# The seven-product scheme moved from the down to the up projection of a convolutional feed-forward block

## The chip, the cores and the metric

The kernel runs on one core of a Trainium2 chip. A core has a matrix engine (TensorE, PE in the rows, with its weight loads as PEld), a vector engine (VectorE, DVE), a scalar engine (ScalarE, ACT), a general engine (GpSimd, POOL) and a queue engine (SyncE, SP) that issues the loads. The metric is the device time of one execution in microseconds.

## The reference, cut to what matters

Two layers, 512 tokens on a grid of 8 rows and 64 columns, width 1024. Each layer adds three branches to x: a mixer with two kinds of attention, cross attention over a memory, and the block that the change touches:

```
def conv_ffn(h, w_up, conv_w, conv_b, w_down):       # h (512, 1024), w_up (1024, 2*2816), w_down (2816, 1024)
    u = h @ w_up
    up = pad(u, one token on either side)
    u = up[:-2] * conv_w[0] + up[1:-1] * conv_w[1] + up[2:] * conv_w[2] + conv_b
    gate, val = split(u, 2)
    return (silu(gate) * val) @ w_down

x = x + conv_ffn(rms_norm(x, norm_ffn[l]), ...)      # last step of each of the two layers
```

Everything is float32.

## The kernel before, in words

**Layout.** All activations lie transposed: channels on the 128 partitions, the 512 tokens along a row. The 1024 channels of x are eight tiles `xT[0..7]`. Tokens are in grid order: the eight rows of a grid column lie together (token = column * 8 + row), so the neighbour in the text is 8 places further, except at a column's wrap-around.

**Products.** A float32 operand is split in two parts of a reduced format: `hi` is the rounded value (a cast, always on ACT), `lo` what is left of it (a subtraction, on DVE or POOL). A product is three matmuls, `hi*hi + hi*lo + lo*hi` (`mm3`, `gemm_T`). A weight block arrives as `raw` (three buffers, 512 KB each) by a DMA on SP's queue and is split by `emit_split`; a letter in `weights()` says which engine makes the low part ("P" POOL, "D" DVE, "S" goes to `combined`). `get_w` hands out the blocks in one fixed order and keeps two split ahead.

**The feed-forward block of a layer.** 22 channel blocks j of 128 gate and 128 value channels. For each, `up_project` makes two products over the eight k tiles (2 x 8 x 3 = 48 matmuls of 512 columns) in PSUM banks tagged `sc` and `tr` (two of each), and `up_finish` multiplies both by the norm's row factor `ffn.rep`, adds the convolution (ACT for the middle tap, four DVE steps for the neighbours, two of 504 columns and two of 7), takes SiLU and multiplies gate by value. `up_first` handles the first two blocks, while the statistics of the norm (`stat`, `spread`) are still under way.

The down projection goes in two parts. The channel blocks 0 to 15 go in four groups of four. For each group g and each of four output pairs (m, m+4), `down_halved` multiplies a 2 x 2 block matrix of weights by a 2 x 2 block matrix of activations (two halves of the four blocks by two halves of 256 tokens) with seven products in place of eight: 7 x 2 x 3 = 42 matmuls of 256 columns instead of 24 of 512. For that, `combined` forms four sums of weight quarters on POOL, and splits three quarters (low parts on `LO_A`, DVE) and four sums (low parts on `LO_S`, POOL); `halved` forms four sums of activation halves on DVE. The results are added to `xT` by seven DVE steps. The down products of a group follow five channel blocks behind (`BEHIND`). The blocks 16 to 21 are multiplied plainly at the end by `down` (layer 0, with the next norm's operands made on the way by `close`) and `down_last` (layer 1, with the final norm and the output).

**What sets the order.** Nothing is issued as it is written. `Tape` records each step with its engine, what it reads and writes, and an estimate of its time (`Step.times`). `Tape.plan` runs a list scheduler over the record: PE takes the earliest step of the program that can start, within a reach of 300 steps; the other engines take the step that is due first. The best of some rounds under disturbed times is played, and each engine then runs its list in order. All steps are issued in `play`, so that the profile gives line 395 for nearly all of them: rows are told apart by their tiles. `mm`, `sc` and `tr` are PSUM tags (four, two and two banks), `t` is a pool of 14 temporary rows, `r` one of 23 operand tiles, `raw`, `hi` and `lo` are weight tiles, `xg` the two big tiles of a norm's split operand.

The functions that the change touches:

Of the kernel before, what the change touches and what calls it, by code (L numbers as in the profile page):

```python
# [19 lines left out]
P = 128  # L20
# [12 lines left out]
N_HALVED = [16, 16]  # L33
UPS = [j + (0, 1, -1, 0)[j % 4] if j < max(N_HALVED) else j for j in range(NF)]
# [24 lines left out]
N_RAW, N_W, AHEAD, AHEAD_HELD, N_WARM, N_LATE, N_FIRST = 3, 4, 2, 5, 7, 4, (12, 22)  # L59

# [429 lines left out]
def encoder_kernel(ctx: ExitStack, tc: tile.TileContext, t: dict, out: list):  # L490
# [5 lines left out]
    LO_A, SUMS, LO_S = DVE, POOL, POOL  # L496
# [60 lines left out]
    def combined(raw):  # L557


        hi, lo = [wpool.tile([P, 6, P], F32R, tag=tag, name=nm(tag)) for tag in ("hi", "lo")]  # L560
        shi, slo = rtile((8, P)), rtile((8, P))
        quarter = raw.rearrange("p (n k) c -> p n k c", k=2)
        first, second = tmp((2, 2, P)), tmp((2, 2, P))
        ACT.copy(hi, raw[:, 0:6])
        LO_A.tensor_sub(lo, raw[:, 0:6], f(hi))
        SUMS.tensor_add(first, quarter[:, 0:2], quarter[:, 3:4].to_broadcast([P, 2, 2, P]))
        SUMS.tensor_add(second[:, 0], first[:, 0], quarter[:, 1])
        SUMS.tensor_add(second[:, 1], second[:, 0], quarter[:, 2])
        for v, c in ((first, slice(0, 4)), (second, slice(4, 8))):
            v = v.rearrange("p n k c -> p (n k) c")  # L570
            ACT.copy(shi[:, c], v)
            LO_S.tensor_sub(slo[:, c], v, f(shi[:, c]))
        parts = {}
        for i, n in enumerate(("11", "22", "12")):
            parts[n] = [(hi[:, 2 * i + k], lo[:, 2 * i + k]) for k in range(2)]
        for i, n in enumerate(("s3", "s1", "s2", "s4")):
            parts[n] = [(shi[:, 2 * i + k], slo[:, 2 * i + k]) for k in range(2)]
        return parts

    def emit_split(act=ACT, cuts=2):  # L580
        n = len(ready)
        key, src, nk, ncol, eng = plan[n]
        raw = raws[n]
        raws[n] = None
        if eng == "S":
            ready.append(combined(raw))
            return
# [84 lines left out]

    def load_parameters():
        SP.dma_start(par, t["par"])
        SP.dma_start(qkg, t["qkg"])
        SP.dma_start(gcol, t["gcol"])
# [55 lines left out]
    class Norm:  # L732
# [51 lines left out]
        def spread(self):  # L784
            self.rep = tpool.tile([P, self.n], F32, tag="rep", name=nm("rep"), bufs=1)
            if self.last is None:
# [105 lines left out]
    for l in range(DEPTH):  # L892
# [602 lines left out]
        def up_project(j, side):  # L1495
            pm = ps_t() if side else ps_s()
            gemm_T(pm, get_w(("up", j, side)), ffn.ops, range(KC), 0, KC - 1)
            return pm

        def up_first():  # L1500


            ws, us = [], []
            for side in range(2):
                ws.append(get_w(("up", 0, side)))
                us.append(ps_mm())
                gemm_T(us[side], ws[side], ffn.ops, range(KC - 1), 0, KC - 1)
            for side in range(2):
                gemm_T(us[side], ws[side], ffn.ops, [KC - 1], 0, KC - 1)
                if side == 0:  # L1510
                    ffn.stat()
            us1 = [up_project(UPS[1], 0)]
            ffn.spread()
            up_finish(0, us)
            us1.append(up_project(UPS[1], 1))
            up_finish(UPS[1], us1)

        def up(j):
            up_finish(j, [up_project(j, side) for side in range(2)])

        def up_finish(j, us):
            for side in range(2):
                DVE.tensor_mul(us[side], us[side], ffn.rep)
            cs = []
            for side in range(2):
                ch = side * NF + j
                u = us[side]
                w = [par[:, l, CW + i * 2 * NF + ch : CW + i * 2 * NF + ch + 1] for i in range(3)]
                cc = tmp()
# [11 lines left out]
            if j < N_HALVED[l]:  # L1541
                halved(j, cs[0])
                return
            acts[j] = rpair()
            ACT.copy(acts[j][0], cs[0])
            DVE.tensor_sub(acts[j][1], cs[0], f(acts[j][0]))

        H = S // 2
        quads, shared, waiting = {}, [], {}

        def halved(j, u):


            n = UPS.index(j)
            if n % 4 == 0:
                shared[:] = [rtile((2, 2, H))]
            if n % 2 == 0:
                waiting[n + 1] = u
                hl = shared[0][:, n // 2 % 2]
# [335 lines left out]
```

## Time and profile before

| | |
|---|---|
| median of three runs | 1309.4 us (1309.1 to 1310.06) |
| the profiled execution, span from first to last instruction | 1308.6 us, 0.8 us under the median |
| PE busy | 1300.8 us, 99%, 6981 matmuls |
| PEld busy | 1120.7 us, 86% |
| DVE busy | 1054.7 us, 81%, 2011 instructions |
| POOL busy | 807.4 us, 62%, 607 instructions |
| ACT busy | 740.1 us, 57%, 1396 instructions |
| DMA | 137.42 MB, 105 GB/s on the mean |

How to read it: rows of groups give engine, operation, `output<-inputs`, shapes and count, then the busy time in us and the mean of one in ns, then the idle time of that engine just before them and what ended it. Matmul records overlap, as matmuls are pipelined: what one costs in a stream is read from the distance between starts, or from a piece of the chain with its count, and not from the mean of its records. A row of the chain of waits gives start, length and count of a piece. The granted clock of TensorE is full (1.00) throughout.

### The profile page before, as it was taken

The numbers are of one execution on the slowest core, as the hardware profiler recorded it, in microseconds if no ns is written. First come the engines' busy times: TensorE is split into PE (matmuls) and PEld (weight loads), VectorE is DVE, ScalarE is ACT, GpSimd is POOL, SyncE is SP. The second block draws the span as 40 slices with busy tenths as digits, with TensorE's granted clock in tenths as the row PEclk, the third lists the DMA queues.
The fourth block names the chain that finished last, engine by engine and source line by source line (L and its number), as shares of the span: only waits on it lengthen the run. The fifth ranks groups of instructions, "written<-read, shape, count | busy, mean of one in ns | idle before, by whom it ended". The sixth has DMA issues, their size and how long they took to land.

```text
span 1308.6 us, 19680 instructions
## 1 busy us (share of the span) xinstructions
PE 1300.8 (99%) x6981; PEld 1120.7 (86%) x6981; DVE 1054.7 (81%) x2011; ACT 740.1 (57%) x1396; POOL 807.4 (62%) x607
## 2 busy tenths in 40 slices
PE   9999999999999999999999999999999999999998
PEld 7898888888888888888888988888888888888897
DVE  8679996766999998987545898966769999989864
ACT  7777686555545444444537767865645445444442
POOL 4465867627666677773736657774466667777650
PEclk9999999999999999999999999999999999999999
DMA  8752313314323333332355422232133233333321
GB/s 284 217 146 51 111 49 97 97 37 115 94 78 115 111 97 97 101 115 91 105 161 178 127 67 82 65 113 82 49 113 99 96 97 102 108 97 98 102 92 65
DMA packets 42898, 137.42 MB, mean 105 GB/s; under 512 B 5040, under 2 KB 8496, under 8 KB 42800
## 3 DMA queue, kind: packets, MB, share of 16 engines
q1 hardware_dynamic: 42224, 135.51, 34.5%
q8 instruction: 55, 0.90, 0.3%
q10 hardware_dynamic: 576, 0.66, 0.1%
q14 instruction: 43, 0.35, 0.1%
HBM read 126.18 MB, written 2.10 MB: 98 GB/s over the span
## 4 chain that ended last, share of the span: by engine, by line
PE 96%; DMA 1%; POOL 1%; DVE 0%; issue 0%; SPq 0%; ACT 0%; POOLq 0%; DVEq 0%
PE mm L395 50%; PE sc L395 25%; PE tr L395 21%; POOL lo L395 1%; DMA t<-in_rope 1%; DMA r<-r 0%; DMA xT<-in_w 0%; POOL t L395 0%; SPq L395 0%; DVE t L395 0%; DVE s L395 0%; POOL r L395 0%; ACT hi L395 0%; DVE r L395 0%; ACT xg L395 0%
## 5 line engine op out<-in xcount | busy, mean ns | idle before, releaser
L395 POOL TENSOR_TENSOR lo<-raw,hi 128x512 fp32r<-128x512 f32 (+2 forms) x236 | 438.3, 1871 | 303.9 <-ACT hi L395 303.2
L395 ACT CAST hi<-raw 128x512 fp32r<-128x512 f32 (+2 forms) x276 | 219.9, 817 | 185.6 <-PE sc L395 70.0
L395 PE MATMUL mm<-r,hi 128*128 128x512 f32 (+1 forms) x928 | 244.8, 344 | 0.0
L395 PE MATMUL sc<-xg,hi 128*128 128x512 f32 (+1 forms) x740 | 228.8, 390 | 0.5 <-ACT xg L395 0.4
L395 PE MATMUL tr<-xg,hi 128*128 128x512 f32 x672 | 207.1, 389 | 0.0
L395 PEld LDWEIGHTS mm<-r,hi 128*128 128x128 f32 x928 | 162.5, 189 | 21.6
L395 PE MATMUL mm<-r,lo 128*128 128x256 f32 (+1 forms) x496 | 164.7, 332 | 0.0
L395 PEld LDWEIGHTS sc<-xg,hi 128*128 128x128 f32 x740 | 136.6, 188 | 28.2 <-ACT xg L395 0.8
L395 PE MATMUL mm<-r,r 128*128 128x256 f32 (+1 forms) x1064 | 159.2, 291 | 0.0
L395 PEld LDWEIGHTS tr<-xg,hi 128*128 128x128 f32 x672 | 126.0, 188 | 26.1
L395 PEld LDWEIGHTS mm<-r,r 128*128 128x128 f32 x1064 | 142.0, 192 | 3.7
L395 POOL TENSOR_TENSOR r<-t,r 128x512 fp32r<-128x512 f32 x80 | 118.1, 1480 | 42.6 <-ACT r L395 42.2
L395 PE MATMUL sc<-xg,lo 128*128 128x512 f32 (+1 forms) x370 | 143.3, 388 | 0.0
L395 ACT CAST r<-t 128x512 fp32r<-128x512 f32 (+1 forms) x164 | 94.4, 588 | 85.0 <-DVE t L395 68.6
L395 PE MATMUL tr<-xg,lo 128*128 128x512 f32 x336 | 130.7, 389 | 0.0
L395 DVE TENSOR_TENSOR xT<-xT,mm 128x256 f32<-128x256 f32 (+1 forms) x216 | 115.5, 554 | 11.5 <-PE mm L395 5.3
L395 PE MATMUL mm<-xg,hi 128*128 128x512 f32 (+1 forms) x386 | 121.5, 393 | 0.0
L395 DVE TENSOR_TENSOR t<-t,t 128x512 f32<-128x512 f32 (+1 forms) x110 | 114.8, 1063 | 4.9 <-ACT t L395 2.2
L395 PE MATMUL mm<-hi,xg 128*128 128x512 f32 (+1 forms) x384 | 108.4, 358 | 0.0
L395 POOL TENSOR_SCALAR t<-t,s 128x512 f32<-128x512 f32 (+1 forms) x112 | 67.5, 619 | 64.7 <-DVE s L395 59.0
L395 PEld LDWEIGHTS mm<-r,lo 128*128 128x128 f32 x496 | 93.9, 189 | 9.5
L395 DVE TENSOR_TENSOR r<-t,r 128x512 fp32r<-128x512 f32 (+1 forms) x84 | 80.0, 972 | 8.3 <-ACT r L395 8.0
(140 smaller groups left out, 2431.6 us busy)
## 6 DMA issues: line engine op xcount, KB each, us to landing
raw<-in_w SPq DMA_DIRECT2D x207, 512.0 KB, 3.6
r<-r SPq DMA_DIRECT2D x30, 256.0 KB, 3.6
r<-in_bias SPq DMA_DIRECT2D x16, 384.0 KB, 4.9
raw<-in_w SPq DMA_DIRECT2D x8, 384.0 KB, 3.0
r<-in_memT SPq DMA_DIRECT2D x4, 512.0 KB, 7.5
xT<-in_w SPq DMA_DIRECT2D x7, 256.5 KB, 4.7
r<-in_w SPq DMA_DIRECT2D x9, 128.0 KB, 4.2
t<-in_memT SPq DMA_DIRECT2D x4, 256.0 KB, 6.4
```

Of the source, the lines that this page charges most:

```text
L395: call(*args, **kwargs)
```

## The change

- The seven-product scheme leaves the down projection. `down_grouped` multiplies the same groups plainly: for each output pair two banks of 12 matmuls of 512 columns (24), and two additions to `xT`.
- It comes to the up projection of the channel blocks 6 to 21. Block matrix on the left: the weights of gate and value (one dimension) by the lower and upper four k tiles (the other). On the right: the two k halves by the two halves of 256 tokens. Seven products of 4 k tiles x 3 matmuls of 256 columns, 84 in place of 48 of 512. The products accumulate in turns in two banks (`val` and `gate`); between them ACT copies partial results out and DVE adds them. The last product and the finish of a block are put off into the next block (`finish_up`). The value half comes out negated, which the taps in `minus` take back.
- The right-hand operands are built once per layer by `operands`, from x, the gain and the norm's factor (so that no multiplication by `rep` follows in these blocks). Until they are there, the channel blocks 0 to 5 (`N_PLAIN`) go the plain way, with the multiplication.
- A weight block of gate and one of value are loaded as two mixed halves ("A", "B") and become three quarters and four sums of 512 columns in `combined`; all seven low parts are on DVE (`LO_S` goes from POOL to DVE), the four sums on POOL. The down weights now go the plain way, low part on POOL. The plain up weights of the blocks 1 and 2 go to DVE.
- Within the block the tokens are in natural order (line by line), so that a neighbour is one place further and the convolution needs two DVE steps instead of four. The norm's operand is written with a stride, and so are the activations for the down projection, which go back to grid order.
- The activations of the blocks 0 to 15 (but 2 and 3) are kept in the two `xg` tiles, which hold the norm's operand until the plain pairs are done.

The diff, cut to its core:

```diff
-N_HALVED = [16, 16]
-UPS = [j + (0, 1, -1, 0)[j % 4] if j < max(N_HALVED) else j for j in range(NF)]
+N_GROUPED = 16
+N_PLAIN = 6
+def behind(n):
+    return [] if n < N_PLAIN else range(0 if n == N_PLAIN else n - BEHIND, min(n - BEHIND + 1, N_GROUPED))
...
-    LO_A, SUMS, LO_S = DVE, POOL, POOL
+    LO_A, SUMS, LO_S = DVE, POOL, DVE
...
+    def combined(first, second, early):
+        parts = {}
+        for n, v in (("11", first[:, 0:4]), ("12", second[:, 4:8]), ("22", first[:, 4:8])):
+            parts[n] = operand_of(v, rtile((8, P)), LO_A)
+        sums = {n: tmp((4, P)) for n in ("s3", "s1", "s2", "s4")}
+        SUMS.tensor_add(sums["s1"], first[:, 4:8], second[:, 0:4])
+        SUMS.tensor_add(sums["s3"], first[:, 0:4], second[:, 0:4])
+        SUMS.tensor_add(sums["s2"], sums["s3"], first[:, 4:8])
+        SUMS.tensor_add(sums["s4"], sums["s2"], second[:, 4:8])
+        for n, tag in (("s1", "hi"), ("s2", "lo"), ("s4", "hi"), ("s3", "lo")):
+            parts[n] = operand_of(sums[n], rtile((8, P)) if early else wtile(tag), LO_S)
         return parts
...
             hi, lo = self.ops[c]
+            if self.gcol == G_FFN:
+                hi, lo = (v.rearrange("p (r c) -> p c r", r=ROWS) for v in (hi, lo))
+                src = src.rearrange("p (c r) -> p c r", r=ROWS)
...
+        def operands():
+            for c in range(4):
+                xs = []
+                for k in (c, c + 4):
+                    v = tmp()
+                    DVE.scalar_tensor_tensor(lines(v), rows(xT[k]), par[:, l, G_FFN + k : G_FFN + k + 1], rows(ffn.psum),
+                                             op0=ALU.mult, op1=ALU.mult)
+                    xs.append(v)
...
+                ACT.copy(pair(base[0]), b)
+                POOL.tensor_sub(pair(base[1]), b, f(pair(base[0])))
+                ACT.copy(base[2][:, i], a[:, :H])
+                DVE.tensor_sub(base[2][:, 2 + i], a[:, :H], f(base[2][:, i]))
...
+                POOL.tensor_sub(one[:, 0], a[:, :H], a[:, H:])
+                DVE.scalar_tensor_tensor(one[:, 1], one[:, 0], -1.0, b[:, H:], op0=ALU.mult, op1=ALU.subtract)
+                POOL.tensor_sub(two[:, 0], b[:, H:], a[:, H:])
+                DVE.scalar_tensor_tensor(two[:, 1], one[:, 1], -1.0, b[:, :H], op0=ALU.mult, op1=ALU.subtract)
+                hi, lo = rtile((4, H)), rtile((4, H))
+                for n, v in ((0, one), (2, two)):
+                    ACT.copy(hi[:, n : n + 2], v)
+                    DVE.tensor_sub(lo[:, n : n + 2], v, f(hi[:, n : n + 2]))
...
         def up(j):
-            up_finish(j, [up_project(j, side) for side in range(2)])
+            gate, val = ps_s(), ps_t()
+            x, y, v = val[:, :H], gate[:, :H], gate[:, H:]
+            sums, p5 = tmp((2, H)), tmp((H,))
+            product(x, w["11"], "11", True)
+            ACT.copy(sums[:, 0], x)
+            product(y, w["12"], "21", True)
+            finish_up()
+            product(v, w["s1"], "t1", True)
+            ACT.copy(p5, v)
+            product(x, w["s2"], "t2", False)
+            ACT.copy(sums[:, 1], x)
+            product(v, w["s4"], "22", False)
+            DVE.tensor_add(gate, gate, sums.rearrange("p n q -> p (n q)"))
+            product(x, w["s3"], "t3", False)
+            DVE.tensor_add(val[:, H:], x, p5)
+            def last():
+                product(x, w["22"], "t4", False)
+                up_finish(j, [gate, val], True)
+            left.append(last)
...
-                for wi, dst, src in (
-                    (w[0], slice(8, S), slice(0, S - 8)),
-                    (w[0], slice(1, 8), slice(S - 8, S - 1)),
-                    (w[2], slice(0, S - 8), slice(8, S)),
-                    (w[2], slice(S - 8, S - 1), slice(1, 8)),
-                ):
-                    DVE.scalar_tensor_tensor(cc[:, dst], u[:, src], wi, cc[:, dst], op0=ALU.mult, op1=ALU.add)
+                DVE.scalar_tensor_tensor(cc[:, 1:], u[:, : S - 1], w[0], cc[:, 1:], op0=ALU.mult, op1=ALU.add)
+                DVE.scalar_tensor_tensor(cc[:, : S - 1], u[:, 1:], w[2], cc[:, : S - 1], op0=ALU.mult, op1=ALU.add)
...
+            hi, lo = (rows(v) for v in acts[j])
+            ACT.copy(hi, lines(cs[0]))
+            DVE.tensor_sub(lo, lines(cs[0]), f(hi))
...
+        def down_grouped(g, m):
+            wh, wl = get_w(("down", g, m))
+            for i in range(2):
+                pm = ps_mm()
+                for k in range(4):
+                    mm3(pm, wh[:, 4 * i + k], wl[:, 4 * i + k], *acts[4 * g + k], k == 0, k == 3)
+                at = xT[m + 4 * i]
+                DVE.tensor_add(at, at, pm)
...
     def up(j):
-        return [cols(("up", j, i), "w_up", 0, KC, i * D_FF + P * j, P) for i in range(2)]
+        return [cols(("up", j, i), "w_up", 0, KC, i * D_FF + P * j, P, "D" if j in (1, 2) else "P") for i in range(2)]
```

Here `lines` and `rows` view a row of 512 tokens as lines by columns: `lines` one that is in natural order, `rows` one that is in grid order (inner step of 8 elements).

More of the change, by code (lines that the diff above doesn't have):

```diff
@@ L555, in emit_raw, with operand_of, wtile @@
         SP.dma_start(*raw_tile())
[L557 to L572, printed above, removed]
-        parts = {}
[L574 to L577, printed above, removed]
+    def operand_of(v, tile, sub):
+        w = tile.rearrange("p (n k) c -> p n k c", n=2)
+        ACT.copy(w[:, 0], v)
+        sub.tensor_sub(w[:, 1], v, f(w[:, 0]))
+        return [(w[:, 0, k], w[:, 1, k]) for k in range(4)]
+    def wtile(tag):
+        return wpool.tile([P, KC, P], F32R, tag=tag, name=nm(tag))
+    def combined(first, second, early):
+        parts = {}
+        for n, v in (("11", first[:, 0:4]), ("12", second[:, 4:8]), ("22", first[:, 4:8])):
[7 more added lines that the diff above has]
+            parts[n] = operand_of(sums[n], rtile((8, P)) if early else wtile(tag), LO_S)
         return parts
```

221 lines of the change are left out of this document (110 added, 111 removed).

## The prediction

> **What bounds the kernel now.** I read the first part of the page, then the chain that ended last, then its pieces in order of time at the end of each feed-forward block, then the busy time by stage.
>
> ```profile
> span 1308.6 us, 19680 instructions
> PE 1300.8 (99%) x6981; PEld 1120.7 (86%) x6981; DVE 1054.7 (81%) x2011; ACT 740.1 (57%) x1396; POOL 807.4 (62%) x607
> ...
> PE 96%; DMA 1%; POOL 1%; DVE 0%; issue 0%; SPq 0%; ACT 0%; POOLq 0%; DVEq 0%
> ```
> ```profile
> 604.40 5.03 PE mm L395 x42
> 609.44 5.47 PE sc L395 x24
> 614.90 5.44 PE tr L395 x24
> 620.34 32.64 PE mm L395 x144
> ...
> 1266.34 17.27 PE mm L395 x144
> ```
> ```profile
> core 0: us, PE busy (x) PEld busy (x) DVE busy (x) ACT busy (x) POOL busy (x), PEclk, DMA share, GB/s
> 402.00:529.60 127.60, 127.60 (x723) 112.44 (x723) 117.78 (x197) 60.94 (x97) 90.26 (x58) 1.00 0.33 100
> 299.40:620.30 320.90, 320.90 (x1734) 279.33 (x1733) 282.57 (x465) 152.24 (x234) 212.53 (x130) 1.00 0.33 101
> ```
> The chain is 96% TensorE. Its pieces give the price of a matmul in a dense stream: 144 of 512 columns in 32.64 us, so 226.7 ns each; 42 of 256 columns in 604.40 to 609.44, so 120.0 ns (again 119.9 in the 144 at 1266.34). A 256-column matmul costs 0.529 of a 512-column one, its own weight load included. The first block runs from 299.4 to 620.34, 321 us; its 1056 wide and 672 narrow matmuls come to 239.4 + 80.6 = 320.0 us. So no wait of any size lies in it: TensorE is the bound at full clock, VectorE (DVE) follows with 92% in the steady part (402 to 529.6, eight channel blocks of 15.95 us).
>
> **The matmul sum.** Per layer the up projection loses 16 of 22 pairs of 48 wide matmuls and gets 16 times 7 products of 12 narrow ones (1344); the down projection loses 16 times 42 narrow ones (672) and gets 16 times 24 wide ones (384). Net: 384 wide fewer, 672 narrow more, -87.0 + 80.6 = -6.4 us; -12.8 us for two layers. Per block of the steady part TensorE goes from 48 wide + 42 narrow (15.92 us) to 84 narrow + 24 wide (15.52 us). All of it lies on the chain, so it counts in full unless another engine takes over.
>
> **DVE in the steady part.** The rows of the eight blocks:
>
> ```profile
> L395 DVE TENSOR_TENSOR xT<-xT,mm 128x512 f32<-128x512 f32 x25 | 16.6, 684 | 1.2 <-PE mm L395 0.2
> L395 DVE TENSOR_TENSOR lo<-raw,hi 128x768 fp32r<-128x768 f32 x9 | 13.2, 1470 | 0.6 <-issue 0.6
> L395 DVE SCALAR_TENSOR_TENSOR t<-sc,par,t 128x504 f32<-128x504 f32 x17 | 12.5, 738 | 0.3
> L395 DVE SCALAR_TENSOR_TENSOR t<-tr,par,t 128x504 f32<-128x504 f32 x16 | 11.9, 742 | 3.5 <-ACT t L395 3.2
> L395 DVE TENSOR_TENSOR t<-t,t 128x512 f32<-128x512 f32 x8 | 11.7, 1466 | 0.4
> L395 DVE TENSOR_TENSOR r<-t,r 128x512 fp32r<-128x512 f32 x12 | 11.1, 953 | 0.0
> L395 DVE TENSOR_TENSOR xT<-xT,mm 128x256 f32<-128x256 f32 x25 | 10.4, 414 | 0.3
> L395 DVE TENSOR_TENSOR t<-t,t 128x256 f32<-128x256 f32 x12 | 9.8, 872 | 0.2
> L395 DVE TENSOR_TENSOR mm<-mm,t 128x256 f32<-128x256 f32 x16 | 6.8, 428 | 0.3
> L395 DVE TENSOR_TENSOR sc<-sc,rep 128x512 f32<-128x512 f32 x8 | 5.5, 688 | 2.0 <-PE sc L395 2.0
> ...
> L395 DVE SCALAR_TENSOR_TENSOR t<-sc,par,t 128x7 f32<-128x7 f32 x16 | 3.5, 216 | 0.0
> ```
> ```profile
> 417.71 0.68 DVE L395 TENSOR_TENSOR r<-t,r 128x512 fp32r<-128x512 f32 x1
> 418.32 0.95 DVE L395 TENSOR_TENSOR lo<-raw,hi 128x768 fp32r<-128x768 f32 x1
> ```
> Instructions that read PSUM have steady prices (0.69, 0.74, 0.43 for 256 columns). Those with both inputs in SBUF swing: 0.68 undisturbed, 1.47 on the mean of the products `t<-t,t`; 0.95 against 1.47 for 768 columns. Per block today there are about six of these (0.95 + 0.69 + 1.5 x 0.68 + 2.5 x 0.43 = 3.7 us undisturbed, 6.4 measured): 0.44 us of waiting each, while POOL is busy 71% of the time. The means sum to 15.9 us per block and DVE is busy 14.7, because records overlap; I scale sums by 0.926.
>
> Removed per block: two multiplications by `rep`, four 7-column steps, 2.75 widths of operand work, seven additions behind the down products, the 768-column weight remainder. After: a 512 and a 256 addition between products (0.69 + 0.43), four convolution steps (2.96), two down additions (1.37), and nine SBUF-only steps of 512 columns (gate times value, the activation's low part, seven weight remainders, which go to DVE because `LO_S` moves there): 6.2. Sum 11.7, waits 9 x 0.44 = 4.0 at most, 2.8 if they shrink with POOL's share (below). Scaled: 13.4 to 14.5 of 15.52 us. It fits about as it does today.
>
> POOL and ACT:
>
> ```profile
> L395 POOL TENSOR_TENSOR lo<-raw,hi 128x1024 fp32r<-128x1024 f32 x17 | 43.3, 2547 | 18.9 <-ACT hi L395 18.6
> L395 POOL TENSOR_TENSOR t<-raw 128x512 f32<-128x512 f32 x8 | 10.3, 1293 | 5.3 <-DMA raw<-in_w 5.3
> ...
> L395 ACT CAST r<-t 128x512 fp32r<-128x512 f32 x28 | 17.1, 619 | 17.6 <-DVE t L395 12.9 <-POOL t L395 4.8
> L395 ACT CAST hi<-raw 128x1024 fp32r<-128x1024 f32 x16 | 16.8, 1050 | 18.3 <-PE sc L395 14.7 <-issue 2.4 <-PE mm L395 1.1
> L395 ACT COPY t<-mm 128x256 f32<-128x256 f32 x17 | 6.3, 370 | 11.0 <-DVE xT L395 9.3 <-PE mm L395 1.6
> L395 ACT ACTIVATE t<-tr,par 128x512 f32<-128x512 f32 x8 | 6.2, 778 | 2.6 <-DVE tr L395 2.6
> ```
> POOL goes from 11.3 us per block to four sums (5.2) and one split (2.5), 7.7: half the time instead of 71%. ACT gets seven 512-column casts (4.3), one of 1024 (1.05), three copies of partial products (1.1) and the conv, SiLU and cast steps (2.8): 9.3 of 15.5. Both keep slack. The three weight loads per block stay three of 512 KB; two of the three buffers are now held together, for casts and sums of 4.3 to 5.2 us, within the 11.9 us of a block that the landing of 3.6 us leaves:
>
> ```profile
> raw<-in_w SPq DMA_DIRECT2D x207, 512.0 KB, 3.6
> ```
> I cost SP's queue and the two tiny negations of conv taps at nothing; if a raw buffer came late by more than the some 6 us between, the next pair's first product would wait for it.
>
> **The bank turns.** Seven products share two banks: a product may write a bank again only after ACT has copied the last one out. The cover is the product between, 12 x 0.120 = 1.44 us; the copy takes 0.37, and a cast that stands in front of it in ACT's order 0.62 to 1.05. That is at most 1.42 plus a handover. The order is written by the planner, which can put down matmuls (5.44 us per block) or the next pair between. I take nothing, and 0.2 us for each of 64 turns (13 us) as the upper end. The last product waits for a DVE addition instead, with two products of the next pair (2.9 us) in front; hidden while DVE keeps up.
>
> **Six plain pairs.** From 299.4 they give TensorE 12 x 5.44 = 65.3 us. Meanwhile DVE must build the new operands, which need the norm (first fence: the block's first matmul; second: DVE's steps for the norm):
>
> ```profile
> 299.37 0.62 PE L395 MATMUL mm<-xg,hi 128*128 128x512 f32 x2
> ```
> ```profile
> 309.90 0.67 DVE L395 TENSOR_SCALAR s<-tr 32x4 f32<-32x4 f32 x4 [2.29 <-PE tr L395]
> 316.27 0.72 DVE L395 STREAM_TRANSPOSE rep<-tr 128x512 f32<-128x512 f32 x1 [5.70 <-PE tr L395]
> ```
> The norm stands at 317.0 today, with 5.7 us in which DVE waited; the new order asks for it sooner, I take 314 to 317, which leaves 48 to 51 us. Due before the first paired block: four operand sets of 2 x 0.74 + 0.43 + 2 x 0.43 + 2 x 0.69 = 4.15 (16.6), seven weight remainders (4.8), the plain weights of j = 2 (2 x 1.2, extended from the 512 and 768 rows: 2.4), pairs 2 and 3 finished (2 x 5.7), pair 4 out of its banks (4.3): 39.6. With 33 SBUF-only steps at 0.44 (14.5), scaled: 50 us. That just fits; pairs 0, 1 and 5 have to wait for the steady part, which has 1 us of DVE slack in each block. I take 1 us of TensorE idle per layer, bounds 0 and 5.
>
> **Strides.** The operands and activations are now turned from grid to line order: inner steps of 64 elements in the two writes of each norm operand, of 8 in operand building, `rep` and the activations. No row shows a strided operand. Bounds: nothing, or a second step per element. From 738 and 216 ns, an element costs (738 - 216) / 497 = 1.05 ns, so 0.54 us per 512. Same element count, so no gain. I take a value near nothing, because the nearest rows (512 columns, three forms) differ by form and not by pattern. At the upper end: 16 such steps before the first paired block (8 us after scaling), and 8 of the closes ahead of it (4.3). [...]
>
> **End of the block.** The last product of pair 21 comes after the first of the opened down groups. Behind it stand 2 x 15 x 0.2267 = 6.8 us of matmuls (in layer 1, 3 x 15 x 0.120 = 5.4) for value's chain of 0.78 + 1.48 + 0.69 + 0.62 + 0.69 = 4.3. Hidden; if DVE is behind, 1 us each.
>
> **Sum.** 1308.6 - 12.8 + 2 x 1 (plain phase) + 0.5 (turns, ends) = 1298.3 in the profiled span. The median of the runs is 1309.4, 0.8 above that span, so 1299.0.
>
> **Rivals.**
> Small stalls only, as summed: 1296.5 to 1302. For it: the whole block runs today within 1 us of its matmuls with DVE at 92%. Chance 0.55.
> Plain phase overrun: DVE's 50 us come late by 3 to 5 per layer: 1302 to 1306. For it: no margin; against: late parts can slide. 0.10.
> Bank turns: half to all of the 13 us: 1303 to 1309. Against it: an order with reserve for each handover. 0.10.
> Strides at the upper end: 8 + 4 us per layer less some 4 that slide, so +13 to +18: 1309 to 1315. 0.13.
> On the other side: DVE becomes the bound of the paired blocks. Place: the nine SBUF-only steps, seven of them for the same pair whose sums POOL makes at that time. Point: (11.7 + 9w) x 0.926 passes today's 15.92 at w = 0.61 us of waiting each, against 0.44 now. At w = 0.7 a block takes 16.65, +0.73 x 32 = 23 us: 1332. [...] Against it: POOL's share falls. 0.12.
>
> **How the numbers follow.** A measurement here tells 0.2% (2.6 us) from no change. Faster: 0.55 + 0.10 + half of the bank turns 0.05 = 0.70. Same: 0.05 + 0.05 of the strides = 0.10. Slower: 0.08 + 0.12 = 0.20. The range 1296 to 1313 leaves out the DVE bound, the worst of the strides and 0.03 below, 0.18. The likeliest case's own range is 1296.5 to 1302.
>
> **What would show it.** 6981 + 576 = 7557 matmuls; PE busy near 1288; matmuls of 256 columns still 120 ns apart in the pairs (more would break the main term); DVE under 95% in the paired blocks and POOL near half; conv steps at 0.74. Wrong if TensorE idles before the first paired block, if `lo` steps on DVE pass 1.3 us on the mean, or if `xg` writes and reads through strides pass 0.75.

## The result and the profile after

| | median | ratio to before, interval |
|---|---|---|
| before, beside it | 1309.7 us (1309.1 to 1311.6) | |
| changed kernel | 1319.9 us (1318.8 to 1321.0) | 1.0075 [1.0061, 1.0090] |

Slower by 10 us, where 1299.0 was forecast. The profiled execution spans 1316.9 us, 18.6 above the sum's 1298.3. TensorE is busy for 1295.7 us of it, where about 1288 was forecast: 7.7 of the 18.6 us lie there, and 10.9 in more idle time. The first part of the changed kernel's page, and the shares of its chain:

```profile
span 1316.9 us, 20628 instructions
...
PE 1295.7 (98%) x7557; PEld 1137.1 (86%) x7557; DVE 1118.4 (85%) x1805; ACT 811.6 (62%) x1526; POOL 738.6 (56%) x559
...
PE 77%; DVE 19%; issue 2%; ACT 1%; DMA 1%; POOL 0%; SPq 0%; DVEq 0%; ACTq 0%
```
The count of matmuls is the forecast's, 7557. What is new is the chain: 19% of it lies on DVE, before it was nothing. The steady part of the changed kernel, first as pieces of the chain (start, length, what), then as busy time of each engine:

```profile
434.92 5.47 PE mm L400 x24
450.46 5.47 PE mm L400 x24
...
512.62 5.47 PE mm L400 x24
```
```profile
core 0: us, PE busy (x) PEld busy (x) DVE busy (x) ACT busy (x) POOL busy (x), PEclk, DMA share, GB/s
434.80:559.10 124.30, 124.30 (x867) 116.63 (x866) 120.19 (x138) 73.07 (x121) 71.92 (x43) 1.00 0.31 102
```
A block starts every 15.54 us (15.95 before) and TensorE idles nowhere in the eight blocks. The gain is there. Most of it is lost at the entry of the feed-forward block. The same view for the 100 us that hold the entry and the first paired block, of the kernel before and then of the changed one:

```profile
290.00:390.00 100.00, 100.00 (x485) 84.52 (x484) 85.32 (x135) 52.30 (x77) 69.41 (x40) 1.00 0.33 95
```
```profile
290.00:390.00 100.00, 93.99 (x440) 76.24 (x439) 98.62 (x119) 59.92 (x86) 60.27 (x38) 1.00 0.26 83
```
DVE goes from 85% to 99% and TensorE, full before, misses 6 us. Where they are stands in TensorE's instructions in order of time (start, length, instruction, and in brackets the idle time before it and what ended it):

```profile
300.24 0.74 PE L400 MATMUL mm<-xg,hi 128*128 128x512 f32 x2 [1.11 <-DVE xg L400]
...
341.71 0.70 PE L400 MATMUL tr<-xg,hi 128*128 128x512 f32 x2 [1.36 <-DVE t L400]
...
375.56 1.69 PE L400 MATMUL tr<-r,lo 128*128 128x256 f32 x12 [1.53 <-ACT t L400]
378.49 1.20 PE L400 MATMUL mm<-xg,hi 128*128 128x512 f32 x4 [1.24 <-ACT xg L400]
```
The first waits for the norm's operand (`xg`), the second for a bank that plain pairs hold until DVE has read it, the third for the first paired block's copy, the fourth for the first activations. Together they make 5.2 of the 6 us. Layer 1 shows the same places (1.06, 1.38, 1.54 and 1.23 us). And the steps behind them, DVE's and then ACT's groups by shape between 285 and 400 us of the changed kernel (busy us, mean ns of one, idle time before):

```profile
L400 DVE SCALAR_TENSOR_TENSOR t<-xT,par,tr 128x512 f32<-128x512 f32 x8 | 9.4, 1206 | 0.0
L400 DVE SCALAR_TENSOR_TENSOR xg<-mm,par,xg 128x512 fp32r<-128x512 f32 x6 | 6.8, 1155 | 0.0
L400 DVE TENSOR_TENSOR xg<-t,xg 128x512 fp32r<-128x512 f32 x4 | 5.8, 1461 | 0.1
...
L400 DVE TENSOR_TENSOR mm<-mm,rep 128x512 f32<-128x512 f32 x4 | 4.4, 1130 | 0.0
```
```profile
L400 ACT ACTIVATE xg<-mm,par 128x512 fp32r<-128x512 f32 x6 | 7.1, 1216 | 0.0
L400 ACT CAST xg<-t 128x512 fp32r<-128x512 f32 x4 | 4.6, 1202 | 5.1 <-DVE t L400 5.1
```
All of these walk through a strided view, and none stands at the 0.69 or 0.74 us of a plain 512-column step. (The 1461 ns are the mean of three steps of 1176 to 1225 ns and one of 2226, beside which POOL was at work for 1.18 us.) So two theories: the strides make DVE and ACT late at the entry (the rival "Strides at the upper end"), or the strides are covered and the new order or the amount of new work is what stalls (the rival "Plain phase overrun").

### The profile page after: what moved, and what is told of

Same layout as the page of the kernel before. It is cut to its first block, busy times and chain, and to the rows that moved or that the text cites. A ratio compares the mean times of both kernels' runs of the same rounds, so it can differ in the third digit from the quotient of the medians.

```text
span 1316.9 us, 20628 instructions
## 1 busy us (share of the span) xinstructions
PE 1295.7 (98%) x7557; PEld 1137.1 (86%) x7557; DVE 1118.4 (85%) x1805; ACT 811.6 (62%) x1526; POOL 738.6 (56%) x559
## 4 chain that ended last, share of the span: by engine, by line
PE 77%; DVE 19%; issue 2%; ACT 1%; DMA 1%; POOL 0%; SPq 0%; DVEq 0%; ACTq 0%
PE mm L400 47%; PE sc L400 15%; PE tr L400 15%; DVE t L400 7%; DVE r L400 3%; DVE xg L400 2%; DVE lo L400 1%; DVE mm L400 1%; DVE xT L400 1%; DVE sc L400 1%; DVE hi L400 1%; DVE tr L400 1%; ACT r L400 1%; DVE s L400 0%; DMA raw<-in_w 0%
## 5 line engine op out<-in xcount | busy, mean ns | idle before, releaser
L400 PE MATMUL mm<-xg,hi 128*128 128x512 f32 (+1 forms) x898 | 282.3, 393 | 5.1 <-ACT xg L400 2.5
L400 PEld LDWEIGHTS mm<-xg,hi 128*128 128x128 f32 x898 | 164.2, 188 | 39.5 <-DVE xg L400 6.6
L400 PE MATMUL mm<-xg,lo 128*128 128x512 f32 (+1 forms) x449 | 174.9, 389 | 0.0
L400 PE MATMUL sc<-r,r 128*128 128x256 f32 (+1 forms) x760 | 132.9, 309 | 0.0
L400 PE MATMUL mm<-r,lo 128*128 128x512 f32 (+1 forms) x336 | 123.2, 367 | 0.0
L400 PE MATMUL sc<-r,hi 128*128 128x256 f32 (+1 forms) x800 | 113.2, 288 | 0.7 <-ACT t L400 0.7
L400 PEld LDWEIGHTS sc<-r,r 128*128 128x128 f32 x760 | 106.3, 191 | 5.9
L400 PE MATMUL tr<-r,lo 128*128 128x256 f32 x768 | 102.9, 283 | 3.8 <-ACT t L400 3.8
L400 PEld LDWEIGHTS sc<-r,hi 128*128 128x128 f32 x800 | 102.7, 192 | 3.2 <-ACT t L400 2.0
L400 DVE TENSOR_TENSOR r<-raw,r 128x512 fp32r<-128x512 f32 x96 | 102.9, 1083 | 2.0 <-ACT r L400 1.8
```

What stands on the lines that cost most here:

```text
L400: call(*args, **kwargs)
```

## The experiments

All ratios are to the kernel before. In the next three parts and in the last one every engine has the same instructions in the same order as in the changed kernel (in the last: as in the kernel that it is built on), and only the views differ. The parts between have orders of their own; there, the strided and the unstrided kernel with seven plain pairs share one order.

**All strides away.**

```diff
-                hi, lo = (v.rearrange("p (r c) -> p c r", r=ROWS) for v in (hi, lo))
+                hi, lo = (v.rearrange("p (c r) -> p c r", r=ROWS) for v in (hi, lo))
-        rows = lambda v: v.rearrange("p (c r) -> p r c", r=ROWS)
+        rows = lambda v: v.rearrange("p (r c) -> p r c", r=ROWS)
```


> Every strided operand of the feed-forward block becomes contiguous, all else and the order of every engine stays as in the changed kernel; left out: the convolution then takes neighbours in grid order, so its neighbours are other tokens. Theory A (the strides: ACT and DVE steps that the planner counts as 0.65 to 0.75 us take 1.15 to 1.2 us, and what comes late is late for TensorE): the idle TensorE at the block's entry, before value 3 and in the first paired block (some 9 us per layer) goes, 1299 to 1304, ratio to before 0.992 to 0.996. [...]

This kernel leaves out the turn to natural order, so its convolution takes the wrong neighbours; the work is the same. 1303.1 us, 0.9952 [0.9940, 0.9964]: 16.8 us less, with the same instructions in the same order. The groups of this kernel between 285 and 400 us, and its busy time by stage:

```profile
L400 DVE SCALAR_TENSOR_TENSOR t<-xT,par,tr 128x512 f32<-128x512 f32 x8 | 5.7, 739 | 0.0
L400 DVE SCALAR_TENSOR_TENSOR xg<-mm,par,xg 128x512 fp32r<-128x512 f32 x6 | 4.3, 741 | 0.0
...
L400 ACT ACTIVATE xg<-mm,par 128x512 fp32r<-128x512 f32 x6 | 4.1, 676 | 0.1
```
```profile
290.00:390.00 100.00, 98.97 (x481) 83.13 (x480) 97.08 (x129) 59.71 (x93) 62.66 (x39) 1.00 0.27 90
```
Here a stride costs DVE 0.41 to 0.47 us per 512 columns (1155 against 741 ns, 1206 against 739) and ACT 0.54 (1216 against 676). It is no wait for POOL: the strided norm steps of DVE beside which POOL did nothing took 1117 to 1131 ns. DVE's busy share is hardly lower (97%), yet TensorE has 5 of its 6 us back: a busy share cannot tell an engine that is just in time from one that is late.

**Which strides.** One kind made contiguous at a time: the norm operand's writes, the activations, the operand building, and the correction `rep` turned once by its ACT copy (this one leaves nothing out; the other three leave tokens in the wrong order).

```diff
 # norm operand
-            if self.gcol == G_FFN:
-                hi, lo = (v.rearrange("p (r c) -> p c r", r=ROWS) for v in (hi, lo))
-                src = src.rearrange("p (c r) -> p c r", r=ROWS)
 # activations
-            hi, lo = (rows(v) for v in acts[j])
+            hi, lo = acts[j]
 # operand building
-  DVE.scalar_tensor_tensor(lines(v), rows(xT[k]), par[...], rows(ffn.psum),
+  DVE.scalar_tensor_tensor(v, xT[k], par[...], ffn.psum,
 # correction
-                ACT.copy(self.rep, self.psum)
+                ACT.copy(self.rep.rearrange("p (r c) -> p r c", r=ROWS), self.psum.rearrange("p (c r) -> p r c", r=ROWS))
-                    DVE.tensor_mul(lines(pm), lines(pm), rows(ffn.rep))
+                    DVE.tensor_mul(pm, pm, ffn.rep)
```


> Same order; only the 16 writes (8 ACT, 8 DVE) per layer of the norm's operand are contiguous; left out: the plain pairs then see their tokens in the wrong order. Theory A: the 2.7 us of idle per layer at the block's entry go, and DVE comes to the operands 3.3 us earlier per layer: 1308 to 1314. If the entry is a matter of the order and not of the strides: 1317 to 1320.

> Same order; only the activations' two writes per channel block (22 ACT casts of 1.2 us and 22 DVE steps) are contiguous; left out: the down projection then has its tokens in the wrong order. They lie in the paired stretch, where TensorE waits little: theory A expects 1315 to 1319 (only the first paired block and the two ends gain). If strides cost in proportion to their number, wherever they lie (44 of the 90 per layer), half of the 16.8 us that the run without any strides gave: 1311 or less.

> Same order; only the 8 DVE steps per layer that build the new operands from x and the norm are contiguous (1.21 to 0.75 us each, 3.7 us of DVE per layer ahead of the first paired block); left out: the paired blocks then have their tokens in the wrong order. Theory A (DVE time ahead of the first paired block is short, so each us of it counts there): idle of the 5.5 us per layer before value 3 and in the first paired block falls by 2 to 3.7: 1312 to 1316. If the norm factor alone or the entry sets it: 1318 to 1320.

> One part of the strides undone: the norm's row factor is turned once per layer by its ACT copy, so that the 12 multiplications per layer of the plain pairs are contiguous (DVE 1.14 to 0.69 us each, 5.4 us per layer). Theory A: the idle time before value 3 and in the first paired block (5.5 + 0.8 us per layer) falls by about half, that at the entry (2.7 us) stays: 1312 to 1316. [...]

| contiguous | steps per layer | median | ratio, interval |
|---|---|---|---|
| norm operand | 16 | 1315.3 | 1.0031 [1.0019, 1.0043] |
| operand building | 8 | 1316.6 | 1.0045 [1.0033, 1.0057] |
| activations | 44 | 1318.3 | 1.0061 [1.0049, 1.0073] |
| correction | 12 | 1318.2 | 1.0065 [1.0053, 1.0077] |

In per cent of the kernel before, under the changed kernel's 1.0075: 0.44, 0.30, 0.14, 0.10; together 0.98 against 1.23 for all at once. The 24 norm and building steps, all on the way into the block, carry three quarters of the 0.98; the 44 activation steps, most of them in the steady part, carry 0.14, and the correction 0.10, both within the intervals of nothing. The theory expected more from three of them: the norm operand and the building came out between its range and the rival's, the correction above its range of 1312 to 1316; the activations came out as expected. The sizes fit the reading that a late step costs where something waits for it next.

**Turning on TensorE's side.** The operand and the activations are written through, and the matmuls read them with a stride (`turn` views a natural row in grid order; `grid` leaves the bank's order as it is).

```diff
-            gemm_T(pm, w, ffn.ops, ks, 0, KC - 1)
+            gemm_T(lines(pm), w, [tuple(rows(v) for v in op) for op in ffn.ops], ks, 0, KC - 1)
-   mm3(pm, wh[:, 4 * i + k], wl[:, 4 * i + k], *acts[4 * g + k], k == 0, k == 3)
+   mm3(grid(pm), wh[:, 4 * i + k], wl[:, 4 * i + k], *map(turn, acts[4 * g + k]), k == 0, k == 3)
```


> The strides moved from ACT and DVE to TensorE's reading of the moving operand, in the same order on every engine: the norm's operand stays in grid order and the plain up matmuls read it with an inner step of 8 elements; the activations of blocks 0 to 15 stay in line order and the down matmuls read them with an inner step of 64; the row factor is turned once (as in the run before that did this alone). The result is the reference's. Of the strided DVE steps only the 8 of operand building per layer and the 6 activations of blocks 16 to 21 stay. If TensorE reads a strided operand at full rate: 1302 to 1307, ratio 0.994 to 0.998, faster than both kernels. If it pays for strides as ACT and DVE do: 288 + 384 wide matmuls per layer at 1.5 to 2 times 226.7 ns, +150 to +300 us, and the matmul rows of plain up (step 8) and down (step 64) tell which step pays.

1619.4 us, 1.2356 [1.2340, 1.2372]. Two pieces of its chain, 24 matmuls of 512 columns with steps of 32 and of 256 bytes:

```profile
341.03 10.35 PE sc L400 x24
```
```profile
466.02 11.75 PE mm L400 x24
```
431 and 490 ns each in place of 226.7 ns: the expectation for an engine that pays for strides.

**A planner that knows the prices, and plain pairs in grid order.** First the planner's estimate of a strided step is raised; then the six plain pairs stay in grid order, with the four-step convolution there. Both give a new order on the engines.

```diff
+        more = (1.05 if self.engine == E_ACT else 0.85) * n
+        busy, length = busy + more, length + more
```
```diff
-            ACT.copy(hi, lines(cs[0]))
+            ACT.copy(hi, lines(cs[0]) if turned else cs[0])
```


> The changed kernel with one addition: the planner's estimate counts 0.85 ns per element more for a strided DVE step and 1.05 for a strided ACT step; strides stay. Theory A1 (the loss comes from an order made with wrong times): 1303 to 1311, idle before the first paired block under 2 us per layer. Theory A2 (the loss comes from the DVE time that the strides cost, whatever the order): 1315 to 1321, same idle time in other places.

> The six plain pairs per layer in grid order (contiguous norm operands, multiplications and activations; their convolution with four DVE steps again), the paired blocks as in the changed kernel. The result is the reference's. Theory A: the entry loses its 2.7 us of idle per layer, DVE before the first paired block has 12 x 0.45 + 12 x 0.45 us less and 24 x 0.22 more, so about 5 us less per layer: 1305 to 1311, ratio to before 0.996 to 1.001. [...]

1341.9 us (1.0244 [1.0231, 1.0258]) and 1329.7 us (1.0154 [1.0141, 1.0167]): both worse than the changed kernel, and above every range that was expected. In the first TensorE waited 6.20 us for a bank (at 376.26 us) and 5.22 us for the first activations (at 387.44 us). In the second the entry was mended, and then TensorE stood behind the first down products; its instructions there:

```profile
380.43 0.80 PE L400 MATMUL mm<-xg,hi 128*128 128x512 f32 x1 [8.15 <-ACT xg L400]
381.02 2.76 PE L400 MATMUL tr<-r,lo 128*128 128x256 f32 x12
383.58 2.76 PE L400 MATMUL sc<-r,hi 128*128 128x256 f32 x12
```
Twelve narrow matmuls after the wait of 8.15 us take 2.56 us from start to start, not 1.44; the mean granted clock is 0.92 from 370 to 435 us, 1.00 in the 70 us before and the 125 after. The next kernel shows slow matmuls and a lower clock behind its long waits as well.

**Less DVE work by a direct close, and three edits upon it.** On top of the natural correction the attention sums are closed straight into `xT` and the operand is made from `xT`; eight DVE copies per layer go. Upon that: seven plain pairs; the first down products one block later; the plain weights of the blocks 1 and 2 split on POOL. All four have orders of their own.

```diff
-            DVE.tensor_add(pm, pm, xT[c])
-            DVE.tensor_copy(xT[c], pm)
-            self.operand(c, src=pm)
+                DVE.tensor_add(xT[c], xT[c], pm)
+                self.operand(c)
 # seven
-N_PLAIN = 6
+N_PLAIN = 7
 # late down
-    return [] if n < N_PLAIN else range(0 if n == N_PLAIN else n - BEHIND, min(n - BEHIND + 1, N_GROUPED))
+    return [] if n <= N_PLAIN else range(0 if n == N_PLAIN + 1 else n - BEHIND, min(n - BEHIND + 1, N_GROUPED))
 # POOL weights
-  ... P, "D" if j in (1, 2) else "P") ...
+  ... P, "P") ...
```


> Strides stay. Two edits that take work from DVE and leave the result as it is: the copy of the correction in natural order (twelve products per layer contiguous), and the closing of the attention sum straight into the resident columns, where now the sum is made in the bank and copied out (eight DVE copies of 512 per layer at the FFN's entry, about 0.69 us each, 5.5 us per layer). Theory (DVE is the chain of the entry and of the first paired block, about 9 us of TensorE idle per layer): the idle falls by 3 to 5 us per layer, 1308 to 1312 us. Rival (the idle comes from the rows that a step must wait for, not from how much DVE has to do): idle as in the changed kernel, 1316 to 1320 us.

> The kernel with the direct close, and seven plain pairs in place of six. One pair more in plain form costs TensorE 48 x 0.2267 - 84 x 0.120 = 0.8 us per layer, but gives DVE and ACT one more plain pair of time (about 10 us) before the first paired block, against one pair's strided work. Theory (too much DVE work for the time ahead of the first paired block): the stalls of the first paired block (about 4 us per layer in the changed kernel) go, 3 us less than the direct close alone. Rival (the stalls come from how the in-order queues stand, which a pair more does not change): 1.6 us more than the direct close alone.

> The kernel with the direct close, with the first products of the down projection issued one paired block later. Theory (they stand in TensorE's queue ahead of the first paired block's work and wait there for the first activations, 1.2 us per layer, which late DVE and ACT steps write): 2 us less than the direct close alone. Rival (the wait only moves to the next thing that DVE and ACT owe): the same as the direct close within 1 us.

> The kernel with the direct close, with the low parts of two plain pairs' up weights made on POOL in place of DVE (about 5.7 us of DVE per layer moved to POOL at 2.4 us a step). Theory (DVE's amount of work before the first paired block is the bound): 2 to 5 us less than the direct close alone. Rival (POOL's steps then lengthen DVE's, or arrive late for the plain pairs): the same or up to 4 us more.

| | median | ratio, interval |
|---|---|---|
| direct close | 1342.8 | 1.0247 [1.0235, 1.0260] |
| with seven plain pairs | 1318.2 | 1.0077 [1.0057, 1.0098] |
| with late down products | 1344.1 | 1.0261 [1.0249, 1.0274] |
| with weights on POOL | 1333.7 | 1.0190 [1.0175, 1.0205] |

The direct close failed both theories: it ended 22.8 us above the upper end of the rival's range. Its DVE norm steps, its TensorE before a bank of the plain pairs, and its granted clock (the column behind POOL's) after the next wait:

```profile
L400 DVE SCALAR_TENSOR_TENSOR xg<-xT,par,xg 128x512 fp32r<-128x512 f32 x8 | 15.2, 1945 | 0.9 <-ACT xg L400 0.9
```
```profile
355.69 0.73 PE L400 MATMUL tr<-xg,hi 128*128 128x512 f32 x2 [3.79 <-DVE t L400]
...
377.70 1.22 PE L400 MATMUL mm<-xg,hi 128*128 128x512 f32 x2 [3.77 <-ACT xg L400]
378.75 2.93 PE L400 MATMUL tr<-r,r 128*128 128x256 f32 x12
```
```profile
378.00:380.00 2.00, 2.00 (x8) 1.45 (x8) 2.00 (x4) 1.57 (x3) 1.42 (x1) 0.50 0.00 0
380.00:382.00 2.00, 2.00 (x11) 2.00 (x11) 2.00 (x5) 1.02 (x3) 0.96 (x1) 0.50 0.10 12
382.00:384.00 2.00, 2.00 (x11) 2.00 (x11) 2.00 (x4) 1.41 (x3) 0.00 (x0) 0.50 0.64 248
```
With `xT` in place of a bank as source, a norm step has two on-chip operands and takes 1945 ns in place of 1155: 6.3 us more per layer against 5.5 saved. The 1945 are a mean of eight; single steps with both inputs on the chip swing in the kernel before, too (512-column steps `r<-t,r`: 678 ns at 417.7 us, 1778 at 419.8). And TensorE ran at a granted 0.50 after each of the two waits of 3.8 us: after the first for some 3.4 us, an estimate from the means of 0.80, 0.50 and 0.71 in the stretches from 355.6 to 357.5, 359 and 361 us, after the second from 378 to 384 us, with 0.99 in the next two. The waits of up to 1.53 us in the changed kernel did not do that (1.00 in the stretches around them). From which length on a wait does it was not shown.

Of the three edits, the time for one more pair gave 24.6 us back and the lighter DVE 9; moving the wait in TensorE's queue gave nothing (+1.3): the wait moved on to the next bank (3.92 us at 381.01 us), as that rival had it. As the orders differ, these sizes hold the luck of an order too. Why this order met waits of 3.8 us was not settled. The norm steps and the copies that went explain about 1 us per layer. Of the other steps with both inputs on the chip between 285 and 400 us, `r<-t,r` was longer than in the changed kernel (means of 1246 against 885 ns for 512 columns, 1620 against 546 for 256), `t<-t,t` of 256 columns shorter (876 against 1231).

**One more plain pair, with and without strides; the copies on ACT.** The pair more on the natural correction and on the kernel without strides; the eight copies on ACT, with six pairs and with seven.

```diff
-N_PLAIN = 6
+N_PLAIN = 7
 # copies on ACT
-            DVE.tensor_copy(xT[c], pm)
+            (ACT.copy if self.gcol == G_FFN else DVE.tensor_copy)(xT[c], pm)
```

The places that name the last plain pairs follow the number.


> The kernel with the correction in natural order (1318.2 us), with seven plain pairs in place of six. The pair more costs TensorE 0.8 us per layer and gives about 10 us of TensorE work ahead of the first paired block. Theory (too much VectorE work for the time ahead of the first paired block): the 3 to 5 us per layer of idle there goes, 1309 to 1313 us. Rival (single late steps in the in-order queues, whatever the time): 1.6 us more than with six, 1319 to 1321 us.

> The kernel without strides (1303.1 us; it leaves out the same as that one: the conv's neighbours are the grid's) with seven plain pairs. Theory (the pair more pays only where VectorE is late): here it costs its 0.8 us per layer less the 1 us per layer of idle that is left at the first paired block, 1302 to 1305 us. Rival (a pair more helps by itself): 1298 us or less.

> The kernel with the correction in natural order and six plain pairs, with the eight copies of the closed attention sums per layer made on ScalarE in place of VectorE; 5.5 us of VectorE's time per layer go, and no step gets another source. Theory (amount of VectorE work; the direct close lost because its norm steps then read two on-chip operands, 1945 in place of 1155 ns): 3 to 5 us of idle per layer go, 1308 to 1312 us. Rival (taking steps from VectorE does not help, whatever they read): 1317 us or more.

> The same with seven plain pairs, and with the eight copies of the closed attention sums per layer (0.69 us each) made on ScalarE in place of VectorE. Theory (amount of VectorE work): 1305 to 1310 us. Rival (ScalarE's activations then come late, or the order decides): not below the kernel with seven pairs alone.

| kernel | median | ratio, interval |
|---|---|---|
| natural correction, six plain pairs (above) | 1318.2 | 1.0065 [1.0053, 1.0077] |
| the same, seven | 1309.7 | 0.9998 [0.9988, 1.0009] |
| the same, six, copies on ACT | 1321.0 | 1.0083 [1.0070, 1.0097] |
| the same, seven, copies on ACT | 1325.2 | 1.0113 [1.0097, 1.0128] |
| no strides, seven pairs (six: 0.9952) | 1305.1 | 0.9963 [0.9950, 0.9975] |

The pair more gains 8.5 us where the strides are, and without them it gains nothing (+2.0 us, its matmul price of 1.6). So it pays where DVE is late and not where it isn't. That fits the theory of the amount, and the rival of the single late steps, which expected 1319 to 1321 us, is out: with seven pairs the strided kernel stands level with the one before. Six and seven pairs have different orders, so the 8.5 us hold an order's luck as well.

The copies on ACT missed, against the theory of the amount. Pieces of the chain of the six-pair kernel at the entry:

```profile
288.76 1.05 ACT hi L400
289.82 0.97 ACT xT L400 x2
290.79 1.05 ACT t L400 x2
291.83 0.48 ACT xT L400
292.31 1.11 ACT xg L400
...
293.44 1.10 DVE xg L400
```
The chain runs through ACT now: copy, square and high part, and DVE's low part behind the high part. ACT's mean share at the entry (60%) had said that there was room; in the ten microseconds in which sums close, there is none: ACT is busy for 9.14 us from 288 to 298 us and for 9.70 from 298 to 308. A wait of 2.80 us for DVE at 345.05 us was not followed up. With seven pairs, four waits of 1.52, 0.42, 1.19 and 0.77 us between 299.9 and 308.4 us were followed by some 3 us (from 308.76 us on) in which wide matmuls started 0.41 to 0.43 us apart in place of 0.227; the mean granted clock from 290 to 345 us is 0.97. So here a group of short waits was followed by slow matmuls, as the waits of 3.8 us were.

**Strides on the bank's side.** The turned copy of the correction reads its bank with a step of 32 bytes, writes its row through, and took 588 ns, as long as the unturned one. So the norm steps were turned the same way, with six and with seven pairs. Nothing is left out, and the orders are those of the kernels under them.

```diff
-                hi, lo = (v.rearrange("p (r c) -> p c r", r=ROWS) for v in (hi, lo))
-                src = src.rearrange("p (c r) -> p c r", r=ROWS)
+                hi, lo = (v.rearrange("p (r c) -> p r c", r=ROWS) for v in (hi, lo))
+                src = src.rearrange("p (c r) -> p r c", r=ROWS)
```


> The kernel with the correction in natural order (1318.2 us, six plain pairs), with the sixteen norm steps per layer turned the other way: each writes its operand row through and reads its bank with a step of 32 bytes, in place of reading the bank through and writing with a step of 256 bytes. Nothing is left out. Theory (the price is on the on-chip tile's side, banks are read at any step for nothing): steps back to about 745 ns on VectorE and 680 ns on ScalarE, and as much as the kernel with contiguous norm writes won, 0.44%: 1312 to 1314 us. Rival (any step costs, whatever it walks through): 1150 and 1220 ns as now, 1317 to 1319 us.

> The same norm steps in the kernel with the correction in natural order and seven plain pairs (1309.7 us). Theory: the entry's idle (2.5 us per layer there) goes, 1303 to 1307 us, below the kernel before (1309.8). Rival: 1309 to 1311 us.

1310.6 us, 0.9995 [0.9983, 1.0006] with six pairs, 7.6 us less than without this turn and more than expected, and 1305.5 us, 0.9965 [0.9950, 0.9980] with seven, 4.3 us less and as expected. The groups of the kernel with six, and the busy time at the entry of the one with six and of the one with seven:

```profile
L400 DVE SCALAR_TENSOR_TENSOR xg<-mm,par,xg 128x512 fp32r<-128x512 f32 x6 | 4.3, 741 | 0.0
...
L400 ACT ACTIVATE xg<-mm,par 128x512 fp32r<-128x512 f32 x6 | 4.1, 676 | 0.1
```
```profile
290.00:390.00 100.00, 95.60 (x451) 78.98 (x450) 96.82 (x123) 59.29 (x88) 60.91 (x38) 1.00 0.27 90
```
```profile
290.00:390.00 100.00, 99.74 (x475) 83.29 (x474) 97.41 (x127) 60.55 (x90) 63.41 (x38) 1.00 0.31 100
```
Step for step the prices of the unturned kernel (741 and 676 ns), with the same bytes moved to the same places: in these steps the stride costs on the side of the on-chip tile (1155 and 1216 ns), and DVE and ACT read a bank with a step of 32 bytes at the price of one read through. With six pairs the first two waits at the entry are down to 0.17 and 0.18 us, but TensorE still misses 4.4 us in this traced layer, in the first paired block (1.20, 1.52 and 1.24 us); the kernel without the turn, whose traced run lay 2.4 us under its median, missed 3.9 there and 5.8 us at layer 1's entry (900 to 1060 us), where this one misses 2.5. With seven pairs 0.3 is left, and 1305.5 us is level with the 1305.1 of the kernel without strides in the same order: there, the strides that remain cost nothing that shows. The version with seven pairs beats both kernels, the one before by 0.35% and the changed one by about 1.1%. What it still waits for is mostly in the paired blocks (1.39 us at 426.12, 1.41 at 1070.24); two rows of TensorE's waits by releaser (total us, times, longest):

```profile
PE sc L400 <- ACT t L400: 3.1, 3, 1.4
...
PE tr L400 <- DVE t L400: 0.5, 2, 0.3
```

## Why the prediction was wrong

- **The failed step: Strides.** The prediction bounded a strided step between nothing and 0.54 us, and took a value near nothing, "because the nearest rows (512 columns, three forms) differ by form and not by pattern". Rows that hold no stride say nothing for the lower end. The steps measure +0.41 to +0.47 us on DVE and +0.54 on ACT, and with all of them away the kernel takes 16.8 us less. The norm steps show both ends: 1155 and 1216 ns with the strided write, 741 and 676 without.
- **The strides rival** had the mechanism and the size: +13 to +18 us, 16.8 measured. The size is in part luck: it priced 24 DVE steps per layer at 0.54 us, where they cost 0.41 to 0.47, and did not count ACT's. It ended at 1309 to 1315 and the time came out at 1319.9, for two reasons. +13 to +18 on the sum's 1299.0 is 1312 to 1317, so the stated range sits some 2 to 3 us too low; and the base was low as well: without strides the kernel takes 1303.1, not 1299.0.
- **The matmul sum** held where it was read, 15.54 us per paired block against 15.52, 120 ns per narrow matmul. PE's busy time without strides is 1291.4 us where about 1288 was forecast; with the idle that is left, this is the rest of 4 us. Its places stay open.
- **Six plain pairs.** 1 us of idle per layer, bounds 0 and 5. Without strides the 100 us of the entry miss 1.0 us, with them 6.0. The term came out for the work that it counted, "just fits" (its parts were not measured one by one), and so nothing was left for the strides. Two terms that share one reserve were added as if each had its own.
- **DVE in the paired blocks**: 120.19 us in eight blocks, 15.0 each, over the forecast's 14.5 and its mark of 95%. It does not bind: TensorE is busy for all of 124.30 us. That rival did not occur, though the share of 97% alone would suggest it.
- **Bank turns, end of block, SP's queue**: nothing in the eight steady blocks. The stall at 375.56 us is a copy in ACT's queue for a bank turn, but of the late entry: without strides it goes. Outside those eight there are waits for such copies of 0.65 us (at 431.78) and 0.68 us (at 1146.10), more than the 0.5 us that the sum had for turns and ends together.
- **POOL** 58% where half was forecast; convolution steps 0.742 to 0.747, as forecast.

## What to carry to other kernels

Price a changed access pattern before a schedule is laid around it: if no row has the pattern, take the upper end when the engine that pays it is the one without reserve. Put a turn where DVE or ACT reads a bank, and keep the on-chip tile's side of the same step contiguous (here 741 ns against 1155 on DVE, 676 against 1216 on ACT). An engine at 85% that goes to 99% in one stage is read from that stage and from what waits for it; there, more cover (one plain pair, at 0.8 us per layer) was worth more here than moving steps to another engine.

## What the runs showed of the hardware

- fp32 steps of 512 columns through an on-chip tile at 256 or 32 bytes, against the same steps without a stride: DVE from 0.74 up to 1.16 or 1.21 us, ACT from 0.68 up to 1.22; the same step with the stride on a bank's side (32 bytes): 0.741 and 0.676.
- TensorE's moving operand read with a stride: 431 ns (32 bytes) and 490 ns (256 bytes) for 512 columns, against 226.7.
- A DVE step with a strided write and two on-chip sources took 1945 ns on the mean of eight, against 1155 with a bank as one source.
- After a wait of 3.77 us TensorE ran at a granted 0.50 for some 6 us; after 1.53 us it stayed at 1.00; after four waits of 0.42 to 1.52 us within 9 us wide matmuls started 0.41 to 0.43 us apart for some 3 us, against 0.227 (mean granted clock 0.97 from 290 to 345 us).
